# Top-k stage of a hybrid decoder layer: gate matching for four heads per operation, later code sums, a third score buffer, and recurrence tiles that share buffers

## The chip, the cores and the metric

The kernel runs on one core of a Trainium2 chip. The metric is the device time of one execution in microseconds (us). The core has five engines with a queue of instructions each: PE (TensorE: matmuls, and loads of their weights), DVE (VectorE), ACT (ScalarE), POOL (GpSimd) and SP (SyncE, which here issues nearly all DMAs). Each engine takes its instructions in the order in which they were queued; semaphores tie the engines together. An instruction that waits holds up everything that is queued behind it on its engine.

## The reference

One decoder layer over 1056 tokens, 1024 of a prompt and 32 of a sample group:

```python
h = x + concat([rwkv7(z_r), multiscale_pool(z_p)]) @ w_out      # z = rmsnorm(x) @ w_in
q = (rmsnorm(h) @ wq).reshape(.., 8 heads, 2, 128)
s1, s2 = q[..0] @ keys[0].T, q[..1] @ keys[1].T                 # 128 scores each
v1, i1 = top_k(s1, 16);  v2, i2 = top_k(s2, 16)
cand   = v1[:, None] + v2[None, :]                              # 16 x 16 sums
sc, ci = top_k(cand, 16);  expert = i1[ci // 16]*128 + i2[ci % 16]
gate   = softmax(sc)
act    = gelu(u[expert] . xn) * gate                            # xn = rmsnorm(h)
h      = h + sum_k act_k * v[expert_k]                          # 16384 experts
h      = h + (p @ w_ple) * sigmoid(rmsnorm(h) @ w_pg);   y = rmsnorm(h)
```

## The kernel before

All of it is one function, `body`, that traces instructions under a framework. The framework gives tiles their memory from pools, adds every semaphore wait that the reads and writes of a tile ask for, and orders each engine's queue at build time: it walks a model of the machine, and among the instructions that are ready it takes the one traced first. So the order of tracing is a priority, and what is held back in that model (a buffer not yet free, say) lets later work pass. A tile with `bufs=n` has n buffers in turn; tiles with one `tag` share them; a new tile on used memory waits for the last reader of what was there.

The stages, with their lines:

- **Projection** (phase_a, 0 to about 330 us): z = rmsnorm(x) @ w_in, every fp32 matmul as three matmuls of rounded parts.
- **Middle** (about 330 to 1500 us): the recurrence in 16 chunks of 64 tokens (`bchunk`, L451; three chunks in flight, each with its own set of tiles by `slot`), and for four groups of tokens the output projection, the norm, the queries and the scores (`phase_c`, L673; scores go to `sc_d` in HBM), then the top-k of each tile of 128 tokens (`top` and `select`, L744 to L907). A hand-written loop of steps merges three streams: in step s the recurrence of later tokens, `top` for group s-2, and `phase_c` for group s-1. Tokens 0 to 671 go the dense way: `select` goes on to build a table of gates over all 16384 experts (`ab`, `gst`, stored to `g_d`, L883 to L907) on DVE, POOL, PE and ACT. Tokens 672 to 1055 go the gathered way: `select` keeps their indices and gates.
- **Dense experts** (about 1180 to 3220 us): 128 blocks of gelu(u @ xn) (`ublock`, L1113), times the gates (`ugate`), times v (`vblock`). Each block is 48 matmuls of 128x336 into a PSUM tile `pd`, of which there are two, and one ACT Gelu that moves it to SBUF (L1116). The first eight results go to tiles OT0 to OT7 (`otile`, L1093), later ones to three tiles `wt` in turn. Beside them, rows of u and v are gathered for the other tokens (POOL issues, DVE multiplies; L1219 to L1236).
- **Tail** (from about 3220 us): the last gate, norms and stores.

The order around the dense experts' start matters here. When the recurrence is done, its pool `pb` closes and pool `dr` opens on that memory: inputs XH and XL, the weight buffers eraw, ehi, elo, and OT0 to OT5. In the last step `top` for the last dense tile (tokens 544 to 671) is traced to its end, the gate pool `gp` (iota, two `gst` of 16 KB, `e16`, two `ab` of 6 KB) closes, and pool `late` opens on memory that reaches into it: OT6, OT7 and the three `wt`. Then the first eight U blocks (`upre`) are merged with `phase_c` of the last group.

In `top`, each of 16 lists of 128 scores takes five DVE operations (two rounds of max and index and one replace). The lists come in from `sc_d` four at a time (tile `scq`, L754, two buffers). In `select` (L770) 50 sums per head replace the 256 (`cand`, on DVE), and the same 50 sums of indices (`code`, on POOL, L777 to L793) say which expert each is. Eight heads then take six DVE operations each (L798 to L806). The 16 winners come out once in order of score (SC, with positions CI) and once in order of position (K16, with the expert); L840 to L849 match the two, a head at a time: on DVE a 16 by 16 comparison of positions (`oh`, L845), on POOL its product with the gates (L846), on DVE a sum over each row (L848). The two `oh` tiles share the buffers of V12 and I12, in which `top` collects the lists' winners.

`body` runs `top` on nine tiles: at tokens 0, 128, 256 (32 tokens, with the heads spread over the partitions), 288, 416 and 544 for the dense way, then at 672, 800 and 928 for the gathered way.

Of the kernel before, what the change touches and what calls it, by code (L numbers as in the profile page):

```python
# [10 lines left out]
F32 = mybir.dt.float32  # L11
# [5 lines left out]
ALU = mybir.AluOpType  # L17
# [46 lines left out]
def body(ctx, tc, io):  # L64
# [60 lines left out]
    def PTT(out, a, b, op):  # L125
        nc.gpsimd.tensor_tensor(out, a, b, op=op)  # L126
# [318 lines left out]
    def bchunk(c, sp=None):  # L445
# [12 lines left out]
        def q4(name, bufs=1):  # L458
            return v3(wt(name, 256, bufs), 64)
# [36 lines left out]
        lts = q4("lts")  # L496
        ACT(lts, quad(ps), AF.Copy)
        yield
        x0 = q4("x0")
        PTT(x0, lts, bc(nmt[:, 0, :]), op=ALU.mult)  # L500
        yx = wt("yx", 512).rearrange("m (j q t) -> m j q t", j=2, q=4)
        Y, X = yx[:, 0], yx[:, 1]
# [98 lines left out]
        s1 = wt("s1", 4)  # L601
        nc.vector.tensor_reduce(s1, po, axis=AX.X, op=ALU.add)
        TS(s1, s1, -1.0 / HD, None, op0=ALU.mult)
        cen = q4("cen")
        TT(cen, po, s1[:, :, None].to_broadcast([128, 4, 64]), op=ALU.add)
        sq = q4("wn")
        ACT(sq, cen, AF.Square)
# [4 lines left out]
        PTT(cen, cen, s2[:, :, None].to_broadcast([128, 4, 64]), op=ALU.mult)  # L612
        ps = PS(pst)
        turn(quad(ps), cen)
        yo = q4("yo")
        TT(yo, quad(ps), fg, op=ALU.mult)
        PTT(yo, yo, fo, op=ALU.add)
        nc.sync.dma_start(y_d[:, :, pos:pos + tt], yo[:, :, :tt])
# [125 lines left out]
    def top(tk, pos, mt):  # L744
        src = sc_d[TIDX[pos]]
        if mt > TC:
            m, nh, loads = mt, HEADS, [(slice(0, mt), 0)]
        else:
            m, nh = mt * SH, HEADS // SH
            loads = [(slice(g * mt, (g + 1) * mt), 2 * nh * g) for g in range(SH)]  # L750
        V12 = tk.tile([128, HEADS, 2, TOPK], F32, name="V12", bufs=1)
        I12 = tk.tile([128, HEADS, 2, TOPK], U32, name="I12", bufs=1)
        for i in range(2 * nh):
            if i % 4 == 0:  # L754
                sq = tk.tile([128, 4, 128], F32, name="scq", bufs=2)
                for d, j in loads:
                    nc.sync.dma_start(sq[d], src[:mt, j + i:j + i + 4, :])
            s_ = sq[:m, i % 4, :]
            v8, i8 = V12[:m, i // 2, i % 2, :], I12[:m, i // 2, i % 2, :]
            nc.vector.max(v8[:, 0:8], s_)  # L760
            nc.vector.max_index(i8[:, 0:8], v8[:, 0:8], s_)  # L761
            s2 = tk.tile([128, 128], F32, name="s2", bufs=2)
            nc.vector.match_replace(s2[:m], v8[:, 0:8], s_, -BIG)
            nc.vector.max(v8[:, 8:16], s2[:m])
            nc.vector.max_index(i8[:, 8:16], v8[:, 8:16], s2[:m])
            yield
        yield from select(tk, pos, mt, m, nh, V12, I12)


    def select(tk, col, mt, m, nh, V12, I12):  # L770
# [3 lines left out]
            ACT(F12[:m, :nh, i, :], I12[:m, :nh, i, :], AF.Copy, scale=1.0 if i else 128.0)  # L774
        cand = tk.tile([128, HEADS, NCAND], F32, name="cand")
        code = tk.tile([128, HEADS, NCAND], F32, name="code")
        for src, dst, add in ((V12, cand, TT), (F12, code, PTT)):  # L777
            off = 0
            for a, b, w in SEG:
                k = b - a  # L780
                o = dst[:m, :nh, off:off + k * w]
                s1, s2_ = src[:m, :nh, 0, a:b], src[:m, :nh, 1, 0:w]
                if k == 1:
                    s1 = s1.to_broadcast([m, nh, w])
                elif w == 1:
                    s2_ = s2_.to_broadcast([m, nh, k])
                else:
                    o = o.rearrange("p h (k w) -> p h k w", w=w)
                    s1 = s1[:, :, :, None].to_broadcast([m, nh, k, w])
                    s2_ = s2_[:, :, None, :].to_broadcast([m, nh, k, w])  # L790
                add(o, s1, s2_, op=ALU.add)
                off += k * w
        PTT(code[sl], code[sl], iotaC[:m, None, :].to_broadcast([m, nh, NCAND]), op=ALU.add)  # L793
        SC = tk.tile([128, HEADS, TOPK], F32, name="SC")
        CI = tk.tile([128, HEADS, TOPK], U32, name="CI")
        s3 = cand
        for hh in range(nh):
            s_ = cand[:m, hh, :]  # L798
            a8, b8 = SC[:m, hh, 0:8], SC[:m, hh, 8:16]
            nc.vector.max(a8, s_)  # L800
            nc.vector.max_index(CI[:m, hh, 0:8], a8, s_)
            s2 = tk.tile([128, 128], F32, name="s2", bufs=2)
            nc.vector.match_replace(s2[:m, :NCAND], a8, s_, -BIG)
            nc.vector.max(b8, s2[:m, :NCAND])
            nc.vector.max_index(CI[:m, hh, 8:16], b8, s2[:m, :NCAND])
            nc.vector.match_replace(s3[:m, hh, :], b8, s2[:m, :NCAND], -BIG)  # L806
            yield
# [29 lines left out]
        else:  # L837
            gl = keep.tile([128, HEADS, TOPK], F32, name=f"gl{col}")
            idx = keep.tile([128, HEADS, TOPK], I32, name=f"idx{col}")
        oh = {}  # L840
        for h0 in range(nh + 1):
            if h0 < nh:
                sh = [m, TOPK, TOPK]
                oh[h0] = tk.tile([128, TOPK, TOPK], F32, name="oh", tag=("V12", "I12")[h0 % 2])
                TT(oh[h0][:m], cF[:m, h0, :, None].to_broadcast(sh), CF[:m, h0, None, :].to_broadcast(sh), op=ALU.is_equal)  # L845
                PTT(oh[h0][:m], oh[h0][:m], gt[:m, h0, None, :].to_broadcast(sh), op=ALU.mult)  # L846
            if h0:
                nc.vector.tensor_reduce(gl[:m, h0 - 1, :], oh[h0 - 1][:m], axis=AX.X, op=ALU.add)  # L848
            yield  # L849
        TS(idx[sl], KI[sl], NEXP - 1, None, op0=ALU.bitwise_and)  # L850
        tinfo[col] = (idx, gl)
# [240 lines left out]

    def otile(db):  # L1093
        if db not in OT:
            OT[db] = (dr if db < KB - 2 else late).tile([128, ND], F32, name=f"OT{db}")
        return OT[db]

    def wt_tile():
# [320 lines left out]
```

## Time and profile before

| | us |
|---|---|
| median of 3 runs (3324.12 to 3328.54) | 3325.07 |
| the profiled execution | 3330.01 |
| its span, first to last instruction | 3328.3 |
| PE busy | 3125.6 |
| DVE busy | 2581.1 |
| POOL busy | 1701.4 |
| ACT busy | 1130.8 |

Busy time is a sum of durations over the span. In the first 1500 us the engines' shares differ from stage to stage; from there to about 3220 us PE is busy without a gap. In rows of groups, "x66 | 41.2, 641" means 66 instructions, 41.2 us busy, 641 ns each on average, and what follows is the engine's idle time just before them with what ended it. "DVE" after an arrow names the engine, "L845" the line of the kernel. In rows of stretches, the pairs are busy time and number of instructions, then PE's granted clock (1.00 is full speed), the DMA engines' busy share and GB/s.

### The profile page before, as it was taken

Reading aid. Unit: us, or ns where it says so; the run is one execution under the profiler, and the core shown is the slowest. Engines: PE = TensorE matmul, PEld = TensorE weight load, DVE = VectorE, ACT = ScalarE, POOL = GpSimd, SP = SyncE. Lnnn points to the kernel's source line nnn. Section 1 sums busy time; section 2 is a strip of 40 time slices with the busy share of each in tenths; the row PEclk is TensorE's granted clock in tenths of the full one; section 3 lists DMA queues with packets and bytes.
Section 4 is the critical chain, followed back from the end, with each engine's and each line's share of the span. In section 5 each row is a group of like instructions: output and inputs, shape, how many; then the busy total and the mean of one; then the engine's idle time right before and its main releaser. Section 6 shows DMA issues by size and latency. Waiting matters only on the chain.

```text
span 3328.3 us, 66589 instructions
## 1 busy us (share of the span) xinstructions
PE 3125.6 (94%) x26777; PEld 2994.6 (90%) x26777; DVE 2581.1 (78%) x4996; ACT 1130.8 (34%) x1734; POOL 1701.4 (51%) x1399
## 2 busy tenths in 40 slices
PE   8997898977998888999999999999999999999997
PEld 7886787876877787999999999999999999999997
DVE  7775333469598979788898888888888888888966
ACT  6442423434464555331222222122122222222243
POOL 5212232235474464246666665656566566666645
PEclk9999999998998888999999999999999999999998
DMA  3326557856676977559999999999999999999934
GB/s 116 118 86 136 145 140 227 284 174 184 201 220 200 283 241 235 186 186 345 339 346 330 333 346 339 324 341 339 329 340 352 327 330 337 340 325 341 322 108 128
DMA packets 437334, 858.90 MB, mean 258 GB/s; under 512 B 108960, under 2 KB 232096, under 8 KB 432544
## 3 DMA queue, kind: packets, MB, share of 16 engines
q1 hardware_dynamic: 326432, 451.93, 41.8%
q0 software_dynamic: 110592, 402.70, 33.6%
q8 instruction: 210, 3.44, 0.4%
q14 instruction: 100, 0.82, 0.1%
HBM read 733.92 MB, written 120.60 MB: 257 GB/s over the span
## 4 chain that ended last, share of the span: by engine, by line
PE 72%; DVE 15%; DMA 5%; POOL 3%; issue 2%; ACT 2%; SPq 1%; ACTq 0%; DVEq 0%; POOLq 0%
PE pd L1110 54%; PE ps L469 4%; PE ps L218 4%; DVE ab L893 2%; PE ps L652 2%; PE ps L654 2%; PE ps L653 2%; PE ps L301 1%; DVE ab L894 1%; PE ps L904 1%; DVE oh L845 1%; DVE ab L896 1%; DMA scq<-sc_d 1%; DMA row<-u,idx 1%; DVE I L761 1%
## 5 line engine op out<-in xcount | busy, mean ns | idle before, releaser
L1219 POOL DMA_INDIRECT row<-v,idx x384 | 526.5, 1371 | 338.4 <-DVE po L1236 150.9
L1219 POOL DMA_INDIRECT row<-u,idx x384 | 542.2, 1412 | 278.7 <-DVE row L1227 106.8
L1086 ACT ACTIVATE ehi<-eraw 128x1024 fp32r<-128x1024 f32 x278 | 294.6, 1060 | 1106.2 <-PE pd L1110 1019.7
L1110 PE MATMUL pd<-XH,elo 128*128 128x336 f32 x2176 | 513.2, 317 | 3.4 <-DVE elo L1088 2.7
L1110 PE MATMUL pd<-XL,ehi 128*128 128x336 f32 x2176 | 514.2, 317 | 0.0
L1110 PE MATMUL pd<-wh,ehi 128*128 128x336 f32 (+1 forms) x2112 | 504.4, 318 | 8.9 <-DVE tg L1300 6.2
L1110 PE MATMUL pd<-XH,ehi 128*128 128x336 f32 x2176 | 511.7, 316 | 0.0
L1110 PE MATMUL pd<-wh,elo 128*128 128x336 f32 (+1 forms) x2112 | 504.4, 318 | 1.5 <-DVE elo L1088 1.5
L1110 PE MATMUL pd<-wl,ehi 128*128 128x336 f32 (+1 forms) x2112 | 503.5, 317 | 0.3 <-DVE wl L1171 0.2
L1236 DVE SCALAR_TENSOR_TENSOR po<-row,act,po 128x1024 f32<-128x1024 f32 x381 | 488.4, 1282 | 6.8
L1227 DVE SCALAR_TENSOR_TENSOR row<-row,xt 128x1024 f32<-128x1024 f32 x384 | 455.4, 1219 | 11.8 <-DMA row<-u,idx 8.1
L1088 DVE TENSOR_TENSOR elo<-eraw,ehi 128x1024 fp32r<-128x1024 f32 x256 | 316.9, 1238 | 79.6 <-ACT ehi L1086 71.1
L1110 PEld LDWEIGHTS pd<-XH,elo 128*128 128x128 f32 x2176 | 372.5, 188 | 4.5 <-DVE elo L1088 3.1
L1110 PEld LDWEIGHTS pd<-XH,ehi 128*128 128x128 f32 x2176 | 372.1, 189 | 0.4
L1110 PEld LDWEIGHTS pd<-wh,ehi 128*128 128x128 f32 x2112 | 362.8, 188 | 9.9 <-issue 6.8
L1110 PEld LDWEIGHTS pd<-XL,ehi 128*128 128x128 f32 x2176 | 371.1, 188 | 0.2
L1110 PEld LDWEIGHTS pd<-wh,elo 128*128 128x128 f32 x2112 | 362.3, 188 | 2.3 <-DVE elo L1088 2.1
L1110 PEld LDWEIGHTS pd<-wl,ehi 128*128 128x128 f32 x2112 | 362.9, 188 | 1.0 <-DVE wl L1171 0.8
L652 PE MATMUL ps<-hi,whi 128*128 128x256 f32 (+1 forms) x592 | 188.1, 320 | 37.5 <-ACT hi L678 14.7
L1179 DVE TENSOR_TENSOR OT<-pd,OT 128x672 f32<-128x672 f32 x120 | 102.8, 857 | 143.3 <-PE pd L1110 142.6
L905 ACT ACTIVATE gst<-ps 128x512 f32<-128x512 f32 x168 | 174.7, 1089 | 94.6 <-PE ps L904 92.9
L126 POOL TENSOR_TENSOR ab<-ab,e 128x512 f16<-128x512 f16 x110 | 140.1, 1286 | 122.6 <-DVE ab L894 93.3
(428 smaller groups left out, 5434.9 us busy)
## 6 DMA issues: line engine op xcount, KB each, us to landing
eraw<-uT SPq DMA_DIRECT2D x128, 512.0 KB
eraw<-vP SPq DMA_DIRECT2D x128, 512.0 KB
g_d<-gst SPq DMA_DIRECT2D x21, 2048.0 KB
gq<-g_d SPq DMA_DIRECT2D x32, 1344.0 KB
whi<-wc_d SPq DMA_DIRECT2D x108, 256.0 KB
wlo<-wc_d SPq DMA_DIRECT2D x108, 256.0 KB
fdc<-fd SPq DMA_DIRECT2D x16, 896.0 KB
wc_d<-whi SPq DMA_DIRECT2D x40, 256.0 KB
```

Of the source, the lines that this page charges most:

```text
L126: nc.gpsimd.tensor_tensor(out, a, b, op=op)
L218: mm(ps[:, :XW], s[:, k, :], x[:, k, a:b], start=first, stop=last)
L469: mm(o[hs], l[hs], r[hs], start=start, stop=stop)
L652: mm(ps[:, :n], whi[:, kk, :], xhi[:, k, :n], start=k == 0, stop=False)
L905: ACT(st[:, :, t2 + q:t2 + q + 4].rearrange("p e t -> p t e"), v3(ps, 128), AF.Copy, scale=1.0 / GS)
L1086: ACT(hi, raw, AF.Copy)
L1088: sub(lo, raw, hi.bitcast(F32), op=ALU.subtract)
L1110: mm(ps[:, a, :n], w_[:, k, :], x_[:, s:s + n], start=first, stop=last)
L1179: TT(halves(OT[db]), ps[:, :, :NH], halves(OT[db]), op=ALU.add)
L1219: nc.gpsimd.indirect_dma_start(out=r[:m], out_offset=None, in_=io[tab], in_offset=bass.IndirectOffsetOnAxis(ap=idx[:m, hh, k:k + 1], axis=0))
L1227: STT(r[:m], r[:m], 1.0, xt[:m], op0=ALU.mult, op1=ALU.mult, accum_out=pre[:m, k:k + 1])
L1236: STT(po[:m], r[:m], act[:m, k:k + 1], po[:m], op0=ALU.mult, op1=ALU.add)
```

## The change

- **Gate matching**: `oh` holds four heads (for the small tile, its two), 1024 numbers per partition instead of 256, in two buffers of its own. A full tile traces the comparison and the product for heads 0 to 3, the same for heads 4 to 7, and then the two sums. It takes two of each operation instead of eight.
- **Code sums**: the seven sums for `code` and the addition of iotaC are traced in the middle of the heads' loop (after the fourth of eight heads) instead of ahead of it.
- **Scores**: `scq` has three buffers instead of two.
- **Memory**: in the recurrence `x0` takes a buffer of `ltm` (two in turn), `cen` takes that of `lts`, `yo` that of `kbT`. All eight OT tiles come from pool `late`; none from `dr`.

```diff
-        x0 = q4("x0")
+        x0 = q4("ltm", 2)
...
-        cen = q4("cen")
+        cen = q4("lts")
...
-        yo = q4("yo")
+        yo = v3(pb.tile([128, 256], F32, name="yo", tag=f"kbT{slot}"), 64)
...
-                sq = tk.tile([128, 4, 128], F32, name="scq", bufs=2)
+                sq = tk.tile([128, 4, 128], F32, name="scq", bufs=3)
...
-        for src, dst, add in ((V12, cand, TT), (F12, code, PTT)):
+        def pairs(src, dst, add):
             off = 0
...
-        PTT(code[sl], code[sl], iotaC[:m, None, :].to_broadcast([m, nh, NCAND]), op=ALU.add)
+        pairs(V12, cand, TT)
...
         for hh in range(nh):
+            if hh == nh // 2:
+                pairs(F12, code, PTT)
+                PTT(code[sl], code[sl], iotaC[:m, None, :].to_broadcast([m, nh, NCAND]), op=ALU.add)
             s_ = cand[:m, hh, :]
...
-        oh = {}
-        for h0 in range(nh + 1):
-            if h0 < nh:
-                sh = [m, TOPK, TOPK]
-                oh[h0] = tk.tile([128, TOPK, TOPK], F32, name="oh", tag=("V12", "I12")[h0 % 2])
-                TT(oh[h0][:m], cF[:m, h0, :, None].to_broadcast(sh), CF[:m, h0, None, :].to_broadcast(sh), op=ALU.is_equal)
-                PTT(oh[h0][:m], oh[h0][:m], gt[:m, h0, None, :].to_broadcast(sh), op=ALU.mult)
-            if h0:
-                nc.vector.tensor_reduce(gl[:m, h0 - 1, :], oh[h0 - 1][:m], axis=AX.X, op=ALU.add)
+        hb = min(4, nh)
+        ohs = []
+        for h0 in range(0, nh, hb):
+            hs, sh = slice(h0, h0 + hb), [m, hb, TOPK, TOPK]
+            oh = tk.tile([128, hb, TOPK, TOPK], F32, name="oh", bufs=2)
+            TT(oh[:m], cF[:m, hs, :, None].to_broadcast(sh), CF[:m, hs, None, :].to_broadcast(sh), op=ALU.is_equal)
+            PTT(oh[:m], oh[:m], gt[:m, hs, None, :].to_broadcast(sh), op=ALU.mult)
+            ohs.append((hs, oh))
+            yield
+        for hs, oh in ohs:
+            nc.vector.tensor_reduce(gl[:m, hs, :], oh[:m], axis=AX.X, op=ALU.add)
             yield
...
-            OT[db] = (dr if db < KB - 2 else late).tile([128, ND], F32, name=f"OT{db}")
+            OT[db] = late.tile([128, ND], F32, name=f"OT{db}")
```

## The prediction

> **What bounds the kernel now.** First the page: the span, the engines' busy time, its slices and the shares of the chain of work that ended last.
>
> ```profile
> span 3328.3 us, 66589 instructions
> ...
> PE   8997898977998888999999999999999999999997
> ...
> DVE  7775333469598979788898888888888888888966
> ...
> PE pd L1110 54%; PE ps L469 4%; PE ps L218 4%; DVE ab L893 2%; PE ps L652 2%; PE ps L654 2%; PE ps L653 2%; PE ps L301 1%; DVE ab L894 1%; PE ps L904 1%; DVE oh L845 1%; DVE ab L896 1%; DMA scq<-sc_d 1%; DMA row<-u,idx 1%; DVE I L761 1%
> ```
>
> A slice is 83 us. From slice 18 on PE is full, and 54% of the chain is one line, the dense experts' matmuls. No part of the change is in that stretch, so it cannot shorten it; it can only change **when PE becomes full, and how much of the dense work is done by then**. Next, the busy time in stretches of the middle stage.
>
> ```profile
> core 0: us, PE busy (x) PEld busy (x) DVE busy (x) ACT busy (x) POOL busy (x), PEclk, DMA share, GB/s
> 840.00:900.00 60.00, 53.03 (x777) 48.12 (x777) 19.22 (x40) 22.82 (x44) 19.45 (x24) 0.91 0.76 216
> 900.00:1173.00 273.00, 234.98 (x3173) 203.29 (x3171) 250.84 (x839) 152.20 (x250) 154.52 (x146) 0.91 0.77 234
> 1194.00:1320.00 126.00, 108.17 (x841) 100.99 (x840) 122.23 (x505) 66.91 (x93) 71.35 (x71) 0.87 0.69 217
> 1312.00:1380.00 68.00, 60.23 (x426) 57.00 (x426) 47.63 (x151) 29.29 (x42) 20.79 (x13) 0.92 0.74 252
> 1380.00:1460.00 80.00, 79.72 (x517) 79.72 (x518) 76.71 (x435) 27.24 (x38) 15.61 (x28) 1.00 0.27 83
> ```
>
> DVE is 92% busy from 900 to 1173 us and 97% from 1194 to 1320 us: top-k and gate building of the last three dense tiles set the pace there. From 840 to 900 us it is 32% busy; the next group's scores are late, and DVE time saved ahead of this gap is worth little. At 1380 us PE is full. The matmuls of the dense experts by stretch:
>
> ```profile
> core 0: us, PE busy (x) PEld busy (x), PEclk, DMA share, GB/s
> 1160.00:1205.00 45.00, 17.38 (x102) 16.16 (x102) 0.75 0.91 301
> 1205.00:1280.00 75.00, 40.43 (x234) 37.42 (x234) 0.92 0.64 198
> 1280.00:1340.00 60.00, 0.00 (x0) 0.00 (x0) 0.79 0.86 268
> 1340.00:1380.00 40.00, 24.53 (x148) 22.75 (x148) 1.00 0.65 240
> 1380.00:1460.00 80.00, 79.72 (x517) 79.72 (x518) 1.00 0.27 83
> ```
>
> 102 + 234 = 336 matmuls, seven blocks of 48, run ahead of 1280 us, **while DVE sets the pace: free filling for PE**. Then none for 60 us. Why they stop is in ACT's timeline: the sixth and seventh Gelu, and the last gate eviction between them.
>
> ```profile
> 1244.32 0.71 ACT L1116 ACTIVATE OT<-pd 128x672 f32<-128x672 f32 x1
> ...
> 1323.67 1.06 ACT L905 ACTIVATE gst<-ps 128x512 f32<-128x512 f32 x1 [0.50 <-PE ps L904]
> ...
> 1335.44 0.74 ACT L1116 ACTIVATE OT<-pd 128x672 f32<-128x672 f32 x1
> ```
>
> OT0 to OT5 lie in `dr`, on the recurrence's memory, and were written by 1244 us. OT6 lies in `late`, on the gate pool's, and came 91 us later, once the last gates were out. The next blocks had no PSUM tile and stood.
>
> **The change, part by part.**
>
> *Gate matching.* The groups of now, and the nearest rows for four heads (1024 numbers per partition):
>
> ```profile
> L126 POOL TENSOR_TENSOR oh<-oh,gt 128x256 f32<-128x256 f32 x66 | 61.1, 934 | 57.7 <-DVE oh L845 57.7
> L845 DVE TENSOR_TENSOR oh<-cF,CF 128x256 f32<-128x256 f32 x66 | 41.2, 641 | 1.6 <-ACT cF L822 0.3
> L848 DVE TENSOR_REDUCE gl<-oh 128x16 f32<-128x256 f32 x66 | 26.6, 407 | 7.6 <-POOL oh L126 7.6
> ...
> L1088 DVE TENSOR_TENSOR elo<-eraw,ehi 128x1024 fp32r<-128x1024 f32 x256 | 316.9, 1238 | 79.6 <-ACT ehi L1086 71.1 <-PE pt L1264 5.2 <-issue 1.6
> L126 POOL TENSOR_TENSOR elo<-eraw,ehi 128x1024 fp32r<-128x1024 f32 x22 | 54.2, 2470 | 45.1 <-ACT ehi L1086 45.0
> ```
>
> A full tile costs DVE 8 x (641 + 407) ns = 8.4 us now. I take 1.24 us for both long operations: 2 x (1.24 + 1.24) = 5.0 us, a saving of 3.4 us or 41%. If time scaled with size (4 x 641 and 4 x 407 ns) nothing would be saved. On POOL 8 x 0.93 = 7.5 us become 2 x 2.5 = 4.9 us. From the first comparison to the last sum the new chain is 1.2 + 2.5 + 2.5 + 1.2 = 7.4 us, no longer than eight steps of about 1 us now. What a saving is worth, the chain says, over 660 to 1340 us and over the last dense tile:
>
> ```profile
> by line: DVE ab L893 10.7%; PE ps L469 5.4%; DVE ab L894 5.2%; PE ps L652 4.5%; PE ps L904 4.3%; PE pd L1110 4.2%; PE ps L654 4.2%; PE ps L653 4.0%; issue 3.4%; DVE ab L896 3.3%; DVE oh L845 3.0%; DMA whi<-wc_d 2.9%; DVE h L709 2.6%; DMA wl
> ...
> by line: PE pd L1110 15.2%; DVE ab L893 11.7%; DMA whi<-wc_d 8.5%; PE ps L904 7.2%; DVE oh L845 5.9%; DVE ab L894 5.4%; PE ps L652 4.6%; DVE h L709 4.4%; PE ps L653 4.2%; PE ps L654 4.2%; DVE ab L896 3.6%; issue 2.8%; DVE gl L848 2.8%; DVE
> ```
>
> 3.0% of 680 us is 20.4 us of comparisons on the chain; the sums stand to them as 2.8 to 5.9, so 30 us for both, and 41% of that is **12 us** (0 to 14). The three gathered tiles' share falls after 1340 us, where PE is filling up and the saving is worth nothing.
>
> *Scores.* DVE's waits for a list of scores:
>
> ```profile
>   DMA scq<-sc_d: 22.6, 8
> ...
>   DMA scq<-sc_d: 17.9, 4
> ```
>
> The second row is the part from 660 to 1340 us. Some of it waits for scores just stored, which no buffer mends; I take **5 us** of 0 to 18. The third buffer adds no DMA; SP's queue only gets some of the same 36 issues earlier, and no wait.
>
> *Code sums.* The same POOL instructions, queued later:
>
> ```profile
> L126 POOL TENSOR_TENSOR code<-F 128x64 f32<-128x64 f32 (+10 forms) x63 | 24.6, 426 | 86.5 <-ACT F L774 86.5
> ...
> L126 POOL TENSOR_TENSOR code<-code,iotaC 128x400 f32<-128x400 f32 x8 | 11.3, 1407 | 0.3
> ...
> L805 DVE FIND_INDEX8 CI<-SC,s 128x8 uint32<-128x50 f32 x66 | 13.4, 203 | 0.0
> ```
>
> Per tile 7 x 0.43 + 1.41 = 4.4 us. Four heads of six operations of 0.2 us, 4.8 us of DVE work, are left behind which they hide. Without that cover a tile's K16 (L811) waits up to 4.4 us, and whatever POOL has queued behind them waits as now. I take nothing, within 4.4 us per tile on the last three, 13 us either way.
>
> *Shared recurrence tiles.* `cen` and `yo` take buffers whose readers finished steps before; the next chunk of the slot needs them only steps after its start. `x0` adds a tenant to `ltm`. POOL already waits there:
>
> ```profile
>   PE ps L469: 122.2, 27
> ```
>
> 27 waits ahead of `ltm`, 4.5 us each, with other streams' POOL work queued behind. A wait for x0's readers joins the sixth part of that traffic. POOL is 57% busy from 900 to 1173 us, which covers it: nothing, at worst some five waits of 4.5 us, 22 us, if the cover were gone.
>
> *OT0 to OT5 to `late`.* By the tiles' sizes: the recurrence pool loses 9 tiles of 1 KB; the top-k pool gains 10 KB (two `oh` of 4 KB, one `scq` of 2 KB) and shifts the gate pool up; `dr` without OT0 to OT5 is 70 KB. `late` (11 tiles of 2688 bytes) must lie directly below `dr`, and its top 8 KB are the three `wt`. All eight OT then lie on the gate pool: OT0 to OT2 on a `gst`, the others on `e16` and `ab`. So what the trace shows for OT6 holds for all: **the first Gelu waits until the last dense tile's gates are nearly out**. Two blocks fill the two PSUM tiles; the other five of the seven leave the free stretch. Queued behind the waiting Gelu on ACT are gate evictions and copies of queries, for which PE and SP wait, if the order built is wrong; I count nothing for that.
>
> Price: 5 x 48 = 240 matmuls at 79.72/517 = 0.154 us each, 37 us of PE time, moved to where PE is full or nearly so. Against it stand the 68.0 - 60.2 = 7.8 us that PE is idle from 1312 to 1380 us, and what `phase_c` gains where these blocks no longer stand between its matmuls:
>
> ```profile
> 1240.00:1312.00 72.00, 18.60 (x60) 12.52 (x60) 0.81 0.68 212
> ```
>
> 60 of its steps of three matmuls in 72 us. Ten us of lead (a little over one block's PE time, an estimate) are 8 steps, about 3 us at 0.12 us per matmul; the weights for the blocks not loaded (5 x 512 KB) free the DMA queues for as much again. I take 6 us. Loss: 37 - 8 - 6 = **23 us**, within 0 (something else fills PE fully) and 37.
>
> *Sum:* -12 - 5 + 23 = **+6 us** on the profiled execution's 3330.0 us, 3336; that execution stands 4.9 us above the median of 3325.1, so **3331 us**.
>
> **The rivals.** *Faster: the filling is not missed.* From 1205 to 1312 us the output projection and queries of the last group take PE's place and end early, so that at 1312 us nearly all of the 37 us find room before 1380 us. For it: PE has 40 us of dense work in 1205 to 1280 us that stood between them. Against: DMA is at 0.86 from 1280 to 1340 us, with no dense matmul there, and PE did not get on faster. If the loss falls to 9 us and the scores give 9: -12 - 9 + 9 = -12, 3313 us. It decides once the loss is under 17 us.
>
> *Slower: the long POOL products hold DVE.*
>
> ```profile
> 1158.81 1.19 POOL L126 TENSOR_TENSOR ab<-ab,e 128x512 f16<-128x512 f16 x1 [1.98 <-DVE ab L894]
> 1159.02 2.06 DVE L893 TENSOR_TENSOR ab<-iota,e 128x2048 f16<-128x2048 f16 x1
> ...
> 1161.72 1.22 DVE L893 TENSOR_TENSOR ab<-iota,e 128x2048 f16<-128x2048 f16 x1
> ```
>
> The same comparison takes 1.22 us alone and 2.06 us where it started beside a POOL product: it ends about as late as if it had begun at that one's end. Products of 2.5 us would then hold gate building's comparisons up to 4.9 us per tile, more than the 3.4 us saved. Gain 2 instead of 12: -2 - 5 + 23 = +16, 3341 us. The Trainium skill, page "SBUF — State Buffer", section "Who interferes with whom", has this as a rule: a DVE instruction with two SBUF inputs and a GpSimd instruction that reads SBUF exclude each other for the whole instruction. The trace agrees (2.06 against 1.22 us); by that rule alone the sum would be +16. Against the rival: eight products of 0.93 us hold as long in all, and max, index and sums go on beside them.
>
> *No effect:* the queues are rebuilt, gain and filling shift alike, and steps end with the mixer as at 840 to 900 us: 3325 us.
>
> **How the numbers follow.** Less than 0.2% (6.65 us) cannot be told from no change. Forecast 45%, its own range 3319 to 3343: 2 faster, 22 same, 21 slower. Faster rival 28%: 26 faster, 2 same. POOL rival 17%, all slower. No effect 10%: 1, 8, 1. In all faster 0.29, same 0.32, slower 0.39. The range takes in most of both rivals: 3306 to 3350.
>
> **What would show it.** Right: `oh` on DVE near 1.2 us and `gl` near 1.2 us, 17 of each; the last gate eviction 10 to 25 us earlier than 1323.7 us; the first Gelu only then, with about 96 dense matmuls ahead of it; PE without a gap from there. Wrong: Gelus at 1190 us as now, or `oh` at 2.5 us, or dense matmuls that start late while PE is full by 1340 us anyway.

## The result, and the profile after

| | us |
|---|---|
| changed kernel, median of 4 runs (3360.01 to 3362.13) | 3360.58 |
| kernel before in the same comparison, median | 3326.81 |
| ratio | 1.0103, 95% interval 1.009 to 1.0116 |

The change costs 34 us (30 to 39). Forecast were 3331 us, within 3306 to 3350: the kernel became slower, as the forecast's sum had it, but by about six times as much. First the page of the changed kernel: span, busy time, PE's slices.

```profile
span 3359.3 us, 66431 instructions
...
PE 3132.5 (93%) x26777; PEld 3002.1 (89%) x26777; DVE 2578.1 (77%) x4898; ACT 1121.6 (33%) x1729; POOL 1696.7 (51%) x1350
...
PE   8998897978888767999999999999999999999997
```

PE has as much to do as before (3125.6 us), and the span is 31 us longer: PE stands idle longer, in the slices ahead of the dense experts' full stretch. DVE's total fell by only 3.0 us (from 2581.1). Now the groups of the matching, and two groups of gate building beside them (busy, mean ns of one, idle time before them):

```profile
L900 DVE TENSOR_TENSOR ab<-iota,e 128x2048 f16<-128x2048 f16 x84 | 126.8, 1516 | 33.1 <-PE ps L911 22.3 <-ACT e L886 9.3 <-POOL ab L126 1.2
L126 POOL TENSOR_TENSOR oh<-oh,gt 128x1024 f32<-128x1024 f32 (+1 forms) x17 | 51.2, 3032 | 57.6 <-DVE oh L850 57.6
L855 DVE TENSOR_REDUCE gl<-oh 128x64 f32<-128x1024 f32 (+1 forms) x17 | 19.9, 1169 | 0.0
L850 DVE TENSOR_TENSOR oh<-cF,CF 128x1024 f32<-128x1024 f32 (+1 forms) x17 | 19.4, 1182 | 0.3 <-ACT cF L827 0.2
L864 DVE TENSOR_SCALAR ci<-idx 128x128 int32<-128x128 int32 (+1 forms) x12 | 11.7, 976 | 0.0
```

The two DVE groups of the matching took 41.2 + 26.6 = 67.8 us and take 19.4 + 19.9 = 39.3 us. Those 28.5 us were saved as forecast (3.4 us per full tile). But DVE's total shows 3.0 of them. In part that is a matter of counting. The records of neighbouring instructions overlap a little, and busy time counts an overlap once; count times mean, summed over all of DVE's groups, falls by 14 us (2868 to 2854), the matching's own two groups by 29. So some 15 us came back as longer records of other operations. Two groups of before, and two of e4, a kernel without any matching (see below):

```profile
L893 DVE TENSOR_TENSOR ab<-iota,e 128x2048 f16<-128x2048 f16 x84 | 120.6, 1443 | 15.2 <-PE ps L904 9.6 <-POOL ab L126 3.1 <-POOL lo L126 1.6
...
L857 DVE TENSOR_SCALAR ci<-idx 128x128 int32<-128x128 int32 (+1 forms) x12 | 6.6, 553 | 0.4 <-ACT e L858 0.4
```

```profile
L886 DVE TENSOR_TENSOR ab<-iota,e 128x2048 f16<-128x2048 f16 x84 | 124.7, 1490 | 20.2 <-PE ps L897 15.4 <-ACT e L872 3.8 <-POOL yo L126 0.6
L850 DVE TENSOR_SCALAR ci<-idx 128x128 int32<-128x128 int32 (+1 forms) x12 | 2.6, 220 | 0.2
```

The same 12 shifts of indices take 5.1 us more, and in e4, without the matching's products, 4.0 us less than before. So there POOL's products hold DVE. The same 84 comparisons of gate building take 6.2 us more, but they take 124.7 us in e4 too, where there is no product to hold them; those 6 us can't be put down to the matching. The timeline of the changed kernel around one tile's matching shows the holding (start, us, engine, line; an "x2" row spans two instructions):

```profile
1054.26 2.35 DVE L850 TENSOR_TENSOR oh<-cF,CF 128x1024 f32<-128x1024 f32 x2
...
1055.55 5.62 POOL L126 TENSOR_TENSOR oh<-oh,gt 128x1024 f32<-128x1024 f32 x2 [2.30 <-DVE oh L850]
...
1056.53 2.42 DVE L864 TENSOR_SCALAR ci<-idx 128x128 int32<-128x128 int32 x1
...
1058.87 2.84 DVE L901 TENSOR_TENSOR ab<-ab,e 128x1024 f16<-128x1024 f16 x1
```

After the comparisons DVE gets two instructions done up to 1061.7 us. The first, a shift of 128 numbers per partition, takes 2.42 us (0.22 us on average in e4); the second takes 2.84 us, where its group's mean is 0.84 us, and ends 0.5 us behind the products' end (1061.2). The last dense tile shows which operations are held and how long the matching is:

```profile
1227.62 2.34 DVE L850 TENSOR_TENSOR oh<-cF,CF 128x1024 f32<-128x1024 f32 x2
1228.90 3.39 POOL L126 TENSOR_TENSOR oh<-oh,gt 128x1024 f32<-128x1024 f32 x1 [2.93 <-DVE oh L850]
1229.88 0.22 DVE L864 TENSOR_SCALAR ci<-idx 128x128 int32<-128x128 int32 x1
1230.08 0.28 DVE L765 FIND_INDEX8 I<-V,s 128x8 uint32<-128x128 f32 x1
...
1232.26 2.34 POOL L126 TENSOR_TENSOR oh<-oh,gt 128x1024 f32<-128x1024 f32 x1
1232.40 2.28 DVE L864 TENSOR_SCALAR ci<-idx 128x128 int32<-128x128 int32 x1
...
1235.92 5.60 DVE L709 SCALAR_TENSOR_TENSOR h<-h,vecs,rstd 128x256 f32<-128x256 f32 x8
...
1241.91 1.20 DVE L855 TENSOR_REDUCE gl<-oh 128x64 f32<-128x1024 f32 x1
```

The first product's record begins while the second comparison is still running, to 1229.96 us, and is 3.39 us long; the second product takes 2.34 us. The difference, 1.05 us, is what was left of that comparison. So a product of four heads takes 2.34 us by itself, and we infer that the first really began at 1229.96 us: DVE holds POOL just as POOL holds DVE. Of the 16 products of four heads 4 took 2.34 to 2.36 us and 12 took 3.3 to 4.0. The shift of indices takes 0.22 us where it comes just ahead of that real start, and 2.28 us beside the second product. A FIND_INDEX8 beside a product takes its usual 0.28 us.

From the first comparison to the last sum it is 1243.1 - 1227.6 = 15.5 us; forecast were 7.4, and this tile took 11.9 us before. The products end 7.0 us after the start, close to the forecast's 6.2; then 5.6 us of the mixer's norm (L709) stand in DVE's queue ahead of the second sum. This tile is an exception: over all nine tiles these stretches add up to 102.7 us, 135.1 before. So the matching itself became shorter, and the kernel slower all the same.

Next the dense experts' matmuls by stretch, and ACT's timeline where they begin in earnest.

```profile
1160.00:1205.00 45.00, 19.02 (x96) 17.48 (x96) 0.88 1.01 327
1205.00:1280.00 75.00, 0.00 (x0) 0.00 (x0) 0.74 0.61 195
1280.00:1340.00 60.00, 12.19 (x65) 12.19 (x66) 0.77 0.72 228
...
1380.00:1460.00 80.00, 69.65 (x440) 67.72 (x441) 1.00 0.38 126
```

```profile
1323.80 1.92 ACT L912 ACTIVATE gst<-ps 128x512 f32<-128x512 f32 x2 [0.71 <-PE ps L911]
...
1327.03 1.35 ACT L1123 ACTIVATE OT<-pd 128x672 f32<-128x672 f32 x2
```

Two blocks, 96 matmuls, run ahead, then none for 75 us; the first Gelu comes at 1327.0 us, behind the last gate eviction. So the OT part went as forecast in its mechanism, to the number of matmuls. But the last eviction is no earlier than before's 1323.7 us, where 10 to 25 us earlier was forecast, and from 1380 to 1460 us the dense experts have 440 matmuls instead of 517: PE is busy for 78.1 of these 80 us, but partly with what is left of the last group's queries and scores.

### The profile page after: what moved, and what is told of

The parts are those of the page before. It is cut to its first block, busy times and chain, and to the rows that moved or that the text cites. A ratio compares the mean times of both kernels' runs of the same rounds, so it can differ in the third digit from the quotient of the medians.

```text
span 3359.3 us, 66431 instructions
## 1 busy us (share of the span) xinstructions
PE 3132.5 (93%) x26777; PEld 3002.1 (89%) x26777; DVE 2578.1 (77%) x4898; ACT 1121.6 (33%) x1729; POOL 1696.7 (51%) x1350
## 3 DMA queue, kind: packets, MB, share of 16 engines
q0 software_dynamic: 110592, 402.70, 33.1%
## 4 chain that ended last, share of the span: by engine, by line
PE 73%; DVE 15%; DMA 5%; issue 2%; ACT 2%; POOL 2%; SPq 1%; ACTq 0%; DVEq 0%; POOLq 0%
PE pd L1117 55%; PE ps L469 5%; PE ps L218 4%; PE ps L652 2%; PE ps L654 2%; PE ps L653 2%; DVE ab L900 1%; PE ps L911 1%; PE ps L301 1%; DMA wlo<-wc_d 1%; DVE s L763 1%; DVE I L765 1%; DVE ab L901 1%; DVE I L761 1%; DMA scq<-sc_d 1%
## 5 line engine op out<-in xcount | busy, mean ns | idle before, releaser
L1226 POOL DMA_INDIRECT row<-v,idx x384 | 548.2, 1428 | 315.4 <-DVE po L1243 149.8
```

The source lines that it names most:

```text
L1226: nc.gpsimd.indirect_dma_start(out=r[:m], out_offset=None, in_=io[tab], in_offset=bass.IndirectOffsetOnAxis(ap=idx[:m, hh, k:k + 1], axis=0))
```

## The experiments

Each kernel was compared with the kernel before. "Worth" below is the difference of two ratios times 3325 us; the interval of one ratio is 3 to 6 us to each side, that of a difference up to 7 or 8.

| run | edit | median us | ratio [95%] |
|---|---|---|---|
| e1_ot_late | before, all OT in `late` | 3348.2 | 1.0075 [1.006, 1.0091] |
| e2_after_ot2 | changed, OT0 and OT1 in `dr` | 3344.1 | 1.0059 [1.0043, 1.0074] |
| e3_match2_ot6 | changed, two heads per operation in the score buffers, OT0 to OT5 in `dr` | 3319.3 | 0.9985 [0.9976, 0.9994] |
| e4_no_match | before, without the matching | 3299.5 | 0.9924 [0.9911, 0.9938] |
| e5_after_hb2 | changed, two heads per operation | 3336.4 | 1.0042 [1.0026, 1.0057] |
| e6_after_scq2 | changed, two score buffers | 3349.1 | 1.008 [1.0064, 1.0096] |
| e7_after_code | changed, code sums early | 3356.1 | 1.0105 [1.0089, 1.0121] |
| e8_match2_ot8 | as e3, all eight OT in `dr` | 3325.6 | 1.0008 [0.9998, 1.0018] |
| f1_pool_halves | changed, products on POOL in halves | 3363.0 | 1.0114 [1.0099, 1.013] |
| f2_steps | changed, eight steps instead of four | 3356.2 | 1.0099 [1.0084, 1.0115] |
| f3_dve_product | changed, product on DVE | 3337.5 | 1.0042 [1.0026, 1.0057] |
| f4_two_heads_dve_product | as e3, product on DVE | 3299.6 | 0.9929 [0.9915, 0.9942] |
| g1_before_dve_product | before, product on DVE | 3297.3 | 0.9918 [0.99, 0.9936] |
| g2_halves_steps | f1 and f2 together | 3356.7 | 1.0099 [1.0084, 1.0113] |
| g3_two_heads_four_steps | as e5, four steps | 3345.7 | 1.0068 [1.0053, 1.0083] |
| g4_share_code | before, shared tiles and later code sums | 3317.2 | 0.9985 [0.9975, 0.9994] |
| h1_dve_product_scq2 | as f3, two score buffers | 3333.8 | 1.0024 [1.0013, 1.0035] |
| h2_share_code_dve_product | as g4, product on DVE | 3309.2 | 0.9947 [0.9933, 0.996] |

### The OT tiles: e1, e2

```diff
# e1, in the kernel before
-            OT[db] = (dr if db < KB - 2 else late).tile([128, ND], F32, name=f"OT{db}")
+            OT[db] = late.tile([128, ND], F32, name=f"OT{db}")
# e2, in the changed kernel
-            OT[db] = late.tile([128, ND], F32, name=f"OT{db}")
+            OT[db] = (dr if db < 2 else late).tile([128, ND], F32, name=f"OT{db}")
```

> The kernel before with one line changed: all eight OT tiles from pool late. Filling theory (the five blocks moved behind the last gates are the whole loss, and the rest of the change is worth nothing): 240 matmuls x 0.154 us = 37 us less what idle PE takes up, so +28 to +37 us, 3355 to 3364 us, with 96 dense matmuls ahead of 1280 us and none more until the last gates are out. Rival (long POOL products and the new order of the middle stage carry part of the 34 us): at most +20 us, 3347 us.

> The changed kernel with OT0 and OT1 back in dr (the room that is left there). Filling theory: two blocks more ahead of the last gates, 96 matmuls x 0.154 us = 15 us back: 3346 us, and 192 dense matmuls ahead of 1300 us. If the Gelu's wait is not what decides: 3360 us as it is.

e1 costs 25 us against a forecast of 23. Giving two tiles back to `dr` (e2) regains 15 us of the changed kernel's loss. The dense experts' matmuls of e1 by stretch, its ACT timeline, and on DVE the start of the last group's output projection (L695) and of the last dense tile's matching (L845):

```profile
1160.00:1205.00 45.00, 16.29 (x96) 15.23 (x96) 0.80 0.93 301
1205.00:1280.00 75.00, 0.00 (x0) 0.00 (x0) 0.70 0.64 197
...
1380.00:1460.00 80.00, 75.62 (x481) 74.14 (x482) 1.00 0.35 114
```

```profile
1310.28 1.14 ACT L905 ACTIVATE gst<-ps 128x512 f32<-128x512 f32 x1 [0.34 <-PE ps L904]
...
1315.72 1.35 ACT L1116 ACTIVATE OT<-pd 128x672 f32<-128x672 f32 x2
```

```profile
1176.78 0.76 DVE L695 TENSOR_TENSOR h<-ps,h 128x256 f32<-128x256 f32 x2 [7.81 <-PE ps L654]
...
1209.90 0.76 DVE L845 TENSOR_TENSOR oh<-cF,CF 128x256 f32<-128x256 f32 x2
```

The same 96 matmuls and the same empty 75 us as in the changed kernel. But here the last gates are out at 1311.4 us, 13 us before they were in the kernel before, presumably because the filling blocks are gone from PE. The changed kernel has the same free PE and its last eviction is as late as before, so these 13 us were lost again. That is the second part of the loss.

Where it lies, the same two starts show in the changed kernel (its matching starts at 1227.6 us, see above):

```profile
1197.80 0.76 DVE L695 TENSOR_TENSOR h<-ps,h 128x256 f32<-128x256 f32 x2 [8.53 <-PE ps L654]
```

It is 21 us behind e1 at the output projection, 18 us at the last dense tile's matching, and 14 us at the last gates. So the time is lost ahead of that matching, in the stage of the recurrence and the earlier tiles, and not in it. The stretch ahead of it in the changed kernel (PE, PEld, DVE, ACT and POOL busy):

```profile
900.00:1173.00 273.00, 231.50 (x3201) 204.86 (x3200) 235.84 (x714) 143.55 (x232) 136.67 (x130) 0.91 0.75 233
```

DVE was busy there for 250.84 us before and is busy for 235.84 us now, and the output projection that follows starts at 1197.8 us, where it started at 1183.0: DVE's busy time does not set the pace. The last gate matters for all that comes after. In the eleven kernels with all OT tiles in `late` (the changed one, e1, e5, e6, e7, f1, f2, f3, g2, g3 and h1) it is out between 1300 and 1327 us, and the span ends 2028 to 2037 us after it in every one.

### Is the time of the matching on the path at all: e4

The matching was left out of the kernel before; the gates stay in order of score.

```diff
-        oh = {}
-        for h0 in range(nh + 1):
...
+        ACT(gl[sl], gt[sl], AF.Copy)
+        for h0 in range(nh + 1):
+            yield
```

> The kernel before without gate matching: the gates stay in order of score, so 8 x (0.64 + 0.41) us of DVE and 7.5 us of POOL per tile are left out. If DVE's time in the matching is on the path, as the prediction's sum had it (30 us of chain): -20 to -30 us, 3300 us. If the steps' ends are set by the recurrence and the mixer, as the equal times of the norms (762, 999, 1233 against 766, 1002, 1232 us) suggest: within 8 us of before, 3319 to 3330 us.

It is worth 25 us. So the matching is not free, as the second forecast had it, but costs nearly the 30 us that the prediction read off the chain. Whether it costs them through DVE's time, the next experiments ask.

### Heads per operation: e5, e3, e8

```diff
# e5, in the changed kernel; e3 as well, with tag="scq", bufs=2, two score buffers and OT0 to OT5 in dr
-        hb = min(4, nh)
+        hb = min(2, nh)
...
-            oh = tk.tile([128, hb, TOPK, TOPK], F32, name="oh", bufs=2)
+            oh = tk.tile([128, hb, TOPK, TOPK], F32, name="oh", bufs=4)
# e8: e3, and five constants of the recurrence copied into pb, so that OT0 to OT7 find room in dr
-            OT[db] = (dr if db < KB - 2 else late).tile([128, ND], F32, name=f"OT{db}")
+            OT[db] = (dr if db < 8 else late).tile([128, ND], F32, name=f"OT{db}")
```

> The changed kernel with its memory given back: gate matching for two heads per operation in the scores' buffers, two score buffers, OT0 to OT5 in dr as before; code sums later and shared recurrence tiles stay. Filling theory: 3327 us, within 7 us of before, and seven blocks ahead of 1280 us. Rival (shared recurrence tiles or the later code sums cost): +10 us or more although seven blocks run early.

> The changed kernel with gate matching for two heads per operation (four buffers of half the size: the same memory, so OT lies as it did). The move of OT alone cost 25 us, the whole change 34. Theory: the other 9 to 12 us are the four-head products on POOL (3.3 us each) that hold DVE and put the last tile's gates later; with half as long ones the last gate eviction comes back to about 1312 us and the time to 3345 to 3350 us. Rival (the scores' third buffer or the later code sums put the gates late): 3355 us or more.

> The third experiment's kernel with the recurrence's masks copied into its own pool, which makes room for all eight OT tiles in dr. Filling theory, followed further: the seventh and eighth Gelu no longer wait, one or two blocks more (7 to 15 us of PE time) run before 1340 us, so 3305 to 3315 us. If PE's gaps from 1240 to 1340 us are not to be had by dense blocks (weights come late, their buffers are shared with the queries'): 3319 us as the third experiment.

At the same memory two heads are worth 20 us over four (e5). Without the OT move two heads come out 5 us below the kernel before (e3), and room for the last two OT tiles adds nothing to that (e8 is 8 us slower than e3). But single heads with the same shared tiles and later code sums come out 5 us below as well (g4, next section). The DVE groups of g4 and of e3:

```profile
L850 DVE TENSOR_TENSOR oh<-cF,CF 128x256 f32<-128x256 f32 x66 | 39.1, 610 | 1.6 <-ACT cF L827 0.5
L853 DVE TENSOR_REDUCE gl<-oh 128x16 f32<-128x256 f32 x66 | 26.7, 407 | 6.0 <-POOL oh L126 6.0
```

```profile
L850 DVE TENSOR_TENSOR oh<-cF,CF 128x512 f32<-128x512 f32 x33 | 31.0, 960 | 0.7
L855 DVE TENSOR_REDUCE gl<-oh 128x32 f32<-128x512 f32 x33 | 22.3, 677 | 8.3 <-POOL oh L126 8.3
```

Two heads per operation take 12.5 us off DVE, and the ratio is 0.9985 in both. One thing besides may count against e3: its `oh` tiles share the scores' buffers, and its waits for scores from 660 to 1340 us are 33.1 us, those of g4 22.6.

### The other parts: e6, e7, g4, h1

```diff
# e6 in the changed kernel, h1 in f3
-                sq = tk.tile([128, 4, 128], F32, name="scq", bufs=3)
+                sq = tk.tile([128, 4, 128], F32, name="scq", bufs=2)
# e7, in the changed kernel
         pairs(V12, cand, TT)
+        pairs(F12, code, PTT)
+        PTT(code[sl], code[sl], iotaC[:m, None, :].to_broadcast([m, nh, NCAND]), op=ALU.add)
...
-            if hh == nh // 2:
-                pairs(F12, code, PTT)
-                PTT(code[sl], code[sl], iotaC[:m, None, :].to_broadcast([m, nh, NCAND]), op=ALU.add)
# g4, in the kernel before: of the change only the lines of x0, cen and yo and the other place of the code sums
-        x0 = q4("x0")
+        x0 = q4("ltm", 2)
...
```

> The changed kernel with two score buffers. If the long products are the rest of the loss: no change, 3355 to 3365 us. If the third buffer (score loads queued earlier on SP, ahead of the mixer's weights) is: 3345 to 3350 us.

> The changed kernel with the code sums traced ahead of the heads' loop as before. If the long products are the rest of the loss: no change, 3355 to 3365 us. If the later code sums are (K16 then waits for POOL): 3345 to 3352 us.

> The kernel before with two parts of the change alone: the shared recurrence tiles and the later code sums. Matching by single heads, two score buffers, OT0 to OT5 in dr. Theory as predicted (both cost nothing): 3319 to 3329 us. Rival (POOL waits for x0's readers, or K16 for the code sums): 3330 to 3347 us. The run with two heads per operation (3319.3 us) has the same two parts, so the difference to it is the worth of two heads instead of one.

> The changed kernel with the product on DVE (3337.5 us) and two score buffers instead of three. With POOL's product two buffers were 11.5 us faster than three (3349.1 against 3360.6). If the third buffer costs by itself (scores loaded earlier let the top-k's first rounds pass ahead of work that is wanted sooner): 3322 to 3331 us. If it cost only together with the long matching: 3334 to 3341 us. As predicted (a gain of 5): 3340 to 3345 us.

The place of the code sums is worth nothing that can be told (e7). With the shared tiles it gains 5 us (g4), so neither is part of the loss. POOL's waits ahead of `x0` show that sharing `ltm` added none; the changed kernel:

```profile
POOL ltm L126 <- PE ps L469: 114.5, 36, 13.1
POOL ltm L126 <- ACT lts L497: 91.2, 11, 14.4
```

The first was 122.2 us. The second stood before under the name of `x`:

```profile
POOL x L126 <- ACT lts L497: 90.3, 12, 14.6
```

The third score buffer costs 8 us (e6) and, with the product on DVE, 6 us (h1); each of the two is hardly larger than its interval, but they agree. DVE's waits for scores from 660 to 1340 us, with three buffers and then with two (e6):

```profile
DVE V L760 <- DMA scq<-sc_d: 29.9, 6, 11.8
```

```profile
DVE V L760 <- DMA scq<-sc_d: 35.0, 7, 12.2
```

The buffer takes 5.1 us off these waits, and yet the kernel is slower with it. Against the kernel before, with its two buffers, the waits did not fall at all: they were 17.9 us there. What the buffer makes late elsewhere was not found.

### POOL's part in the matching: f1, f2, g2, g3

The expectations name three theories: the length of one product, the number of steps in the merged loop, and time that scales with size.

```diff
# f1: product in halves
-            PTT(oh[:m], oh[:m], gt[:m, hs, None, :].to_broadcast(sh), op=ALU.mult)
+            for h1 in range(0, hb, 2):
+                PTT(oh[:m, h1:h1 + 2], oh[:m, h1:h1 + 2], gt[:m, h0 + h1:h0 + h1 + 2, None, :].to_broadcast([m, 2, TOPK, TOPK]), op=ALU.mult)
# f2: a second yield behind each comparison and each sum; g2: both
             yield
+            yield
# g3, in e5
-            yield
+            if h0 + hb >= nh or h0 % 4:
+                yield
...
-            yield
+            if hs.stop >= nh or hs.start % 4:
+                yield
```

> The changed kernel with each product on POOL cut in two instructions of two heads; comparisons, sums, steps and memory stay as they are. Two heads per operation throughout took 3336.4 us against 3360.6 us for four. Theory 'length' (one POOL product of 3.3 us holds DVE, and POOL work queued behind it, for too long): most of these 24 us come back, 3336 to 3345 us. Theory 'steps' (with four heads the matching is four steps of the merged loop instead of nine, so the loop traces this stream in another order against phase_c and the recurrence): nothing comes back, 3355 to 3365 us. Theory 'scaling' (an operation over four heads costs four times one over one head): nothing comes back, and the two halves together take as long as one.

> The changed kernel with two steps of the merged loop instead of one after each comparison and after each sum, so eight for a full tile, as with two heads per operation. Operations and memory stay as they are. Theory 'steps': 3336 to 3345 us. Theory 'length': 3355 to 3365 us.

> The changed kernel with both the products on POOL in halves and eight steps instead of four; comparisons and sums stay at four heads. With two heads throughout it took 3336.4 us, each of the two edits alone 3363 and 3356. If the two only work together: 3336 to 3345 us. If it is the finer comparisons and sums (the first product starts after 0.7 instead of 1.2 us, the first sum waits for one product of 1.7 instead of 3.3 us): 3352 to 3365 us.

> Two heads per operation in the changed kernel (3336.4 us) with a step of the merged loop only after every second comparison and sum, so four as in the changed kernel. If the finer operations matter by themselves: 3333 to 3342 us. If it was the number of steps with them: 3352 to 3362 us. If the queues' order as built makes most of the difference between such neighbours: anything from 3336 to 3360 us, and the pair of two and four heads proves little.

Neither halves nor steps nor both give anything back (+4, -1, -1 us). The shortest halves take 1.26 us, the shortest whole products 2.34, so POOL gains hardly anything from size here. With e7 these are four kernels that differ from the changed one in details of order and stay within 4 us of it, so its time does not look like an accident of the queues. Two heads with four steps (g3) lie between: 12 of the 20 us of e5. What in two heads gains those 20 us stays open.

### The product on DVE: f3, f4, g1, h2

One word is changed: the product with the gates goes to DVE.

```diff
# g1, in the kernel before; f3, f4, h2 likewise
-                PTT(oh[h0][:m], oh[h0][:m], gt[:m, h0, None, :].to_broadcast(sh), op=ALU.mult)
+                TT(oh[h0][:m], oh[h0][:m], gt[:m, h0, None, :].to_broadcast(sh), op=ALU.mult)
```

> The changed kernel with the product with the gates on DVE instead of POOL, four heads per operation. DVE takes about 2 x 1.2 us more per full tile, POOL loses 2 x 3.3 us, and no engine waits for the other in the matching. Theory 'length': 3336 to 3345 us, or lower by what the waits cost. Theory 'steps': 3355 to 3365 us. If DVE's own time is what counts: eight tiles by 2.4 us more, of which three on the path, 3360 to 3370 us.

> As the run with two heads per operation in the score buffers and OT0 to OT5 back in dr (3319.3 us), with the product on DVE: 4 x 0.69 us more of DVE per full tile, 4 x 1.5 us less of POOL. Theory 'length': a gain of some us, 3308 to 3317 us. Theory 'steps': 3314 to 3324 us. If DVE's own time is what counts: 3322 to 3328 us.

> The kernel before, one head per operation, with the product with the gates on DVE instead of POOL and nothing else changed. If what costs in the matching is that POOL takes part (its products hold DVE's other operations, and each of the two engines waits for the other): a gain as in the two pairs so far (four heads 3360.6 to 3337.5, two heads 3319.3 to 3299.6), 3300 to 3312 us. If DVE's own time is what counts: 66 x 0.5 us more, a third of it on the path, 3330 to 3340 us.

> The kernel before with the product on DVE (3297.3 us), the shared recurrence tiles and the later code sums; these two alone gave 3317.2 against 3323.8 us. If the gains add: 3287 to 3295 us. If they are the same gain (time of POOL ahead of the recurrence and the gates): 3295 to 3301 us.

| heads per operation | product on POOL | product on DVE | worth | recurrence's last output (L616) starts at |
|---|---|---|---|---|
| one (before, g1) | 1 | 0.9918 | 27 us | 1124.5, then 1111.5 us |
| one, with shared tiles and later code sums (g4, h2) | 0.9985 | 0.9947 | 13 us | 1125.8, then 1115.8 us |
| two (e3, f4) | 0.9985 | 0.9929 | 19 us | 1129.3, then 1107.7 us |
| four (changed, f3) | 1.0103 | 1.0042 | 20 us | 1127.8, then 1110.5 us |

In every layout it gains, and g1 and f4 are 24 to 27 us faster than the kernel before, and 58 to 62 us faster than the changed one. With all of the matching on DVE, g1 is as fast as e4 with none of it. The time of f3 is what theory 'length' forecast, but f1 had already spoken against length. The page of g1 and its groups:

```profile
PE 3115.4 (95%) x26777; PEld 2987.1 (91%) x26777; DVE 2589.9 (79%) x5062; ACT 1128.9 (34%) x1734; POOL 1655.4 (50%) x1333
```

```profile
L846 DVE TENSOR_TENSOR oh<-oh,gt 128x256 f32<-128x256 f32 x66 | 34.6, 553 | 0.0
L845 DVE TENSOR_TENSOR oh<-cF,CF 128x256 f32<-128x256 f32 x66 | 29.1, 477 | 1.1 <-ACT cF L822 0.3
L848 DVE TENSOR_REDUCE gl<-oh 128x16 f32<-128x256 f32 x66 | 24.8, 407 | 0.0
```

DVE takes on 34.6 us of products, and its total rises by 2589.9 - 2581.1 = 8.8 us. So some 26 us of held time would have gone with POOL's products; 12.1 of them show in the comparison itself, 41.2 us before and 29.1 now. Totals tell this only roughly: kernels with the same 4898 DVE instructions (the changed one, e2, e6, e7, f1, f2, g2) have totals from 2560.0 to 2578.1 us. The four-head pair says the same:

```profile
PE 3120.9 (94%) x26777; PEld 2991.1 (90%) x26777; DVE 2574.2 (77%) x4915; ACT 1122.0 (34%) x1729; POOL 1641.4 (49%) x1333
```

f3 puts 17 products on DVE, some 20 us, and DVE is busy 3.9 us less than in the changed kernel. Of POOL's queue g1 takes 61.1 us of products and 57.7 us in which POOL stood waiting for a comparison (the group of before); DVE's 7.6 us of waiting for products go too. As DVE's total hardly moves, it is not DVE's time that g1 gains. It is what POOL's part added: the handing over from engine to engine twice per operation, or the place in POOL's queue, in which gate building and the recurrence stand as well.

Two things on record speak for the second. The matching's own stretches hardly shorten in g1: 127.1 us over the nine tiles for 135.1, and 11.5 for 11.9 in the last dense tile. And where the product leaves POOL, the recurrence ends 10 to 22 us earlier in all four pairs, as the table shows. In g1 the last dense tile's matching starts 17.9 us earlier than before, and its last gates are out 18.8 us earlier, so nearly all of that was gained by then:

```profile
1217.35 0.76 DVE L845 TENSOR_TENSOR oh<-cF,CF 128x256 f32<-128x256 f32 x2
```

```profile
1199.45 0.76 DVE L845 TENSOR_TENSOR oh<-cF,CF 128x256 f32<-128x256 f32 x2 [0.32 <-ACT cF L822]
...
1303.87 2.08 ACT L905 ACTIVATE gst<-ps 128x512 f32<-128x512 f32 x2
```

No run moved only the product's place in POOL's queue, so this is argued and not shown. Another unexplained difference: the gains of g4 and g1 do not add (h2 is 10 us slower than g1).

## Why the prediction was wrong

**OT0 to OT5 to `late`, +23: right in the mechanism, and in the size partly by luck.** e1 measured 25 us alone, with the mechanism as told: 96 matmuls ahead, an empty stretch, the first Gelu behind the last gates. Within it two terms were off and nearly cancel: the gates gained 13 us when the filling left PE, where 6 were counted for the mixer, and the mixer ended later, so that PE came to the dense experts later (481 of their matmuls for 517 from 1380 to 1460 us).

**Gate matching, -12: the step that failed.** The sizes were right or near: 1.18 us for 1.24 on DVE, 2.34 for 2.5 us for a product by itself. (Most products took 3.3 us, as a comparison on DVE held them, so POOL saved 10 of 61 us and not 20 or so.) The error was to take DVE's busy share from 900 to 1173 us for the pace of that stage, and so to turn a share of the chain into time: 41% of the 30 us that comparisons and sums have on the chain. Saving DVE 28.5 us saved nothing, and saving it 12.5 us in e3 saved nothing against g4. The 30 us are real (e4: 25), but they are not DVE's busy time. They are what POOL's part brings about: 13 to 27 us go when DVE does all the work, though it then does more, and 27 us with single heads is as much as leaving the matching out.

**The POOL rival, +16, was the nearest.** It named POOL's products as what takes the saving away. Its rule was the Trainium skill's, page "SBUF — State Buffer", section "Who interferes with whom". The same section says that `tensor_scalar` can take the ports that POOL shares in its fast modes and be blocked for a whole instruction, and that `tensor_reduce` on this chip is not. The trace agrees with the first (0.22 against 2.28 us for the shift of indices); for the second the sums' mean stays at 407 ns with and without POOL's products. But the rival put its price on the gate comparisons, whose longer time can't be put down to the products (e4), and it left the matching a gain of 2 us. The runs show the price elsewhere: the stage ahead of the last dense tile gets longer.

**Scores, -5: wrong.** DVE's waits for scores did not fall from the 17.9 us of before: they are 29.9 us with three buffers and 35.0 with two. The third buffer costs 6 to 8 us.

**Code sums and shared tiles, 0: right**, a gain of 5 us if anything.

Put together from the ratios: +25 (OT, e1) and -5 (shared tiles and code, g4) make 20; the changed kernel stands at 34. The remaining 14 are the third buffer's 8 and about 6 for four heads on POOL, where -17 was forecast for both. With the product on DVE on both sides (f3 against g1) the change costs 41 us, more than the OT tiles' 25, so nothing points to a saving by four heads there either; two heads there (f4) are 6 us ahead of single ones (h2), which is about one interval. The sum over parts measured in different kernels holds to a few us only, as e5, g3 and h2 show. What makes the stage ahead of the last dense tile so late in the changed kernel stays open.

## What to carry to other kernels

When a short chain goes from DVE to POOL and back, try it on one engine before batching it: the work that POOL takes off DVE may come back as held time, and what stands behind it in POOL's queue waits. An engine that is 92% busy need not set the pace: leave the work out, or move it to another engine, before its share of the chain is counted as time to be saved. Find the event on which the rest depends (here the last gate) and see where it was already late. And before a buffer is moved, look at whose memory it lands on and when that is let go: that part could be forecast from the trace of before.

## What was not expected of the hardware

- A POOL product with a repeated operand gains little from size: the shortest took 0.72 us for 256 numbers per partition, 1.26 for 512 and 2.34 for 1024. On DVE the comparison goes from 477 ns (without POOL beside it, g1) to 1182 ns for about four times as much.
- The holding goes both ways, and each engine's record contains it. Beside a comparison on DVE a POOL product took 3.39 us instead of 2.34. POOL's records in a profile are rough, but here the difference is what was left of the comparison, to 0.01 us.
- DVE operations with one input can be held as well: a shift of 128 whole numbers took 2.42 us beside a POOL product. FIND_INDEX8 and TENSOR_REDUCE were not held.
- DVE's busy time contains what it is held by POOL. Moving 34.6 us of work from POOL to DVE raised it by 8.8 us, in totals that differ by up to 18 us between kernels with the same DVE instructions.
